# The second half of an output projection, finished tile by tile in every token group instead of the last group alone

## Chip, cores and metric

The kernel runs on one core of a Trainium2 chip. The metric is the time of one execution on the device, in microseconds (us). A kernel is judged by the median of its runs.

## What is computed

One layer of a streaming encoder: norm, a wide input projection, two parallel branches (gated linear attention, gated spatial mixing), their merge, one output projection with a gated residual add, and a final norm. The change touches the end only:

```
    x = x + gate * (merged @ w_out)                  # merged: (tokens, 1024), w_out: (1024, 1024)
    y = rmsnorm(x, final_norm_w)                     # x * rsqrt(mean(x*x) + EPS) * w, float32
```

There are 2,048 prompt tokens and 128 sample tokens, all in float32.

## The kernel before

**Groups and phases.** The 17 tiles of 128 tokens are worked on in three groups: 6 prompt tiles, the sample tile with 4 prompt tiles, and 6 prompt tiles. Each group goes through the phases `h` (input projection), `a` and `b` (the branches' projections) and `o` (output projection, `w_out`). A phase is a list of blocks, a block a list of jobs, and a job is what TensorE (PE) does with one piece of 128 to 512 weight rows. Every float32 operand is split into a high part (`hi`, a cast by ScalarE, ACT) and a rest (`lo`, a subtraction by VectorE, DVE, or GpSimd, POOL), and a product is three matmuls: hi hi, hi lo, lo hi.

**The output projection.** `P.o` has two blocks of kind N (`NJob`), one for each half of the 1,024 output columns. A block has eight jobs, one for each 128 rows of `w_out`. `NJob.tile(j)` issues the three matmuls of one job for token tile j (lines 394 to 396) and adds them up in that tile's PSUM bank. In the order before, `mm` runs all tiles of a job before the next job, so that all the banks of a block are complete only with job 7. The last block of the program (`blocks[-1]`) is the exception: its jobs 4 to 7 are held back and then run tile by tile, each tile with four jobs one after the other, and each tile is finished at once.

**Emptying a bank.** `out_fin(n)(j, ps)` multiplies the bank by the gate (line 1522, DVE), adds that to the residual x in tile `y` (line 1524, DVE for even j, POOL for odd j), and sums the squares (`y_square`, line 1548, ACT): at once for the first half, and for the second half in the generator `y_gen`.

**Who sets the order.** The order is written by a Python planner. `run_all` goes through the jobs: `flush` empties the banks of the job before, `prepare(n)` issues the casts and subtractions for the weights of the jobs n+2 and n+3, `feed(n)` issues weight loads as far as nine weight buffers reach, `job.mm()` issues the matmuls, and `job.then` holds what follows a job. Each engine executes its own instructions in the order in which they were issued. Work beside the matmuls sits in generators in the list `side`, and `step()` advances the first of them between matmuls. `out_before(0)` drains that list before the output projection.

**Fills of the next group.** In phase `h` the next group needs seven combinations of its operands (`AOPS`, in the order S1, A11, S2, S4, A12, S3, A22), each as hi and lo in a pair of large buffers (`U`, 18 in all). `fill_h` casts each combination (line 160, ACT) and subtracts (line 161, the first half of the columns on DVE, the second on POOL). The fills hang on the `then` lists of the output projection's jobs: behind job 1 of its second half the fourth, behind job 3 the fifth (A12), behind job 5 the sixth (S3), behind job 7 the last (A22). Each of these takes over the buffers of two jobs that have just ended.

**The final norm.** Behind the second half, `out_after` puts `y_gen` in front of the next group's matmuls: one step loads the norm's weights, a step for each tile sums the squares, one step reduces them (line 1563, DVE) and takes the root on POOL (lines 1564 and 1565), and then, one step later, each step scales and stores one tile (`y_out`, line 1543, DVE). The next group's first blocks `ga[0]` and `v` are of kind S (`SJob`): 12 matmuls a job (lines 326 to 328) with seven jobs. Four banks are used; jobs 4 to 6 add to banks that `evac` has first read. That is the copy on ACT (line 338) and the sums on DVE (lines 339 and 342), and `g_fin` (line 1320) takes the results out. Job 4 waits for the copy at 338, job 5 for the sum at 342, job 6 for the sum at 1320 that reads job 5's bank. The sum at 342 is in `SJob.evac`:

```
            elif i == 2:
                bk["u2"] = CT(h)
                dve.tensor_tensor(bk["u2"], bk["Q"], bk["t"], ALU.add)
```

Below, b0 is the first block of the next group, b0.5 its job 5, b1.0 the first job of the next block, which runs between b0.5 and b0.6. The boundary is the moment at which b0.0 starts.

Of the kernel before, what the change touches and what calls it, by code (L numbers as in the profile page):

```python
# [13 lines left out]
ALU = mybir.AluOpType  # L14
# [84 lines left out]
LEAD = 2  # L99
# [8 lines left out]
def _fast_body(tc, nc, ctx, io):  # L108
    pe, act, dve, pool, sync = nc.tensor, nc.scalar, nc.vector, nc.gpsimd, nc.sync
# [53 lines left out]
    def mm(out, lhs, rhs, start=True, stop=True):  # L163

        ops = [(a, b) for n, a in enumerate(lhs) for m, b in enumerate(rhs) if n + m < 2]
        for n, (a, b) in enumerate(ops):
            pe.matmul(out, a, b, start=start and n == 0, stop=stop and n == len(ops) - 1)  # L167
# [214 lines left out]
    class NJob(Job):  # L382
# [5 lines left out]
        def tile(self, j):  # L388
# [6 lines left out]
            pe.matmul(bk[j], a, self.w[:, 1], start=False, stop=False)  # L395
            pe.matmul(bk[j], b, self.w[:, 0], start=False, stop=i == 7)  # L396

        def mm(self):
            blk, nt = self.blk, self.blk.ops.h // 64
            if blk is not blocks[-1] or self.i < 4:  # L400
                for j in range(nt):
                    self.tile(j)
                    if j % 2:
                        step()
            elif self.i == 7:
                for j in range(nt):
                    for job in blk.jobs[4:8]:
                        job.tile(j)
                    blk.fin(j, blk.banks[j])

        def evac(self):
            if self.i == 7 and self.blk is not blocks[-1]:
                for j in range(self.blk.ops.h // 64):
                    self.blk.fin(j, self.blk.banks[j])

    class Blk:


        def __init__(self, kind, src, fin, after=None, before=None):
            self.src, self.fin, self.after, self.before = src, fin, after, before  # L420
            self.raw, self.tmp, self.banks = [], {}, {}
            cls, n = {"S": (SJob, 7), "P": (PJob, 4), "N": (NJob, 8)}[kind]
            self.kind, self.jobs, self.kept, self.num = kind, [cls(self, i) for i in range(n)], False, None
            self.ntiles = 4 if kind == "N" else 2
# [10 lines left out]
    def step():  # L435
        rate[1] += rate[0]
        while rate[1] >= 1.0:
            rate[1] -= 1.0
            side.step()

    blocks, jobs, feed_q, feed_n, staged = [], [], [], [0], set()
# [27 lines left out]

    def feed(n, most=4):  # L470

        own = sum(1 for job in jobs[max(n, 0):max(0, n + LEAD + 2)] if not (job.blk.kind == "S" and job.blk.kept))
        while feed_n[0] < len(feed_q):
            live = [f for f in feed_q[:feed_n[0]] if f[3] > n]
            _, fn, args, _ = feed_q[feed_n[0]]
            raw = sum(1 for f in live if f[2])
            if len(live) + own >= NW or (args and raw >= most):
                break
            fn(*args)
            feed_n[0] += 1  # L480
# [24 lines left out]
    def run_all(first):  # L505
        for n, job in list(enumerate(jobs))[first:]:
            flush()
            if job.i == 0 and job.blk.before:
                job.blk.before()
            prepare(n)  # L510
            keep(n + 1)
            feed(n)
            job.mm()
            last[0] = job
            for fn in job.then:
                fn()


    class Steps:
# [433 lines left out]
    def make_group(g):  # L953

        tiles = groups[g]
        nt = len(tiles)
# [539 lines left out]
        def out_before(n):  # L1496
            def f():
                if n == 0:
                    side.drain()
                    cur["yss"] = sm1.tile([128, NTM, 4], F32, tag="xss", name=nm("yss"))  # L1500
                    cur["y"] = {}
                cs = slice(512 * n, 512 * n + 512)
                if n and g + 1 == NG:
                    cur["yw"] = norm_w()
                cur["gate"] = {}
                for k in sorted({t[0] for t in tiles}):
                    cur["gate"][k] = S(512)
                    sync.dma_start(cur["gate"][k], gate_d[k][:, cs])
                for j in range(0, nt, 3):
                    y = U([3, 512])  # L1510
                    for a, b, src in x_rows(g, 512 * n, 512):
                        a2, b2 = max(a, j), min(b, j + 3)
                        if a2 < b2:
                            sync.dma_start(y[:, a2 - j:b2 - j, :], src[:, a2 - a:b2 - a, :])
                    for i in range(j, min(nt, j + 3)):
                        cur["y"][n, i] = y[:, i - j, :]
            return f

        def out_fin(n):
            def f(j, ps):  # L1520
                t, y = S(512), cur["y"][n, j]
                dve.tensor_tensor(t, ps, cur["gate"][tiles[j][0]], ALU.mult)  # L1522
                final = n and g + 1 == NG
                (pool if j % 2 and not final else dve).tensor_tensor(y, y, t, ALU.add)
                if n == 0 or final:
                    y_square(n, j)
                if final:
                    if j > 0:
                        y_tile(j - 1)
                    if j + 1 == nt:  # L1530
                        y_tile(j)
            return f
# [14 lines left out]
        def y_square(n, j):  # L1547
            act.activation(K1("sq", 512, BF16), cur["y"][n, j], AF.Square, accum_out=cur["yss"][:, j, n:n + 1])
# [6 lines left out]

        def y_gen():
            ws = norm_w()
            for j in range(nt):
                yield
                y_square(1, j)  # L1560
            yield
            r = sm1.tile([128, NTM], F32, tag="xrs", name=nm("yrs"))
            dve.tensor_reduce(r[:, 0:nt], cur["yss"][:, 0:nt, 0:2], AX.X, ALU.add)
            pool.tensor_scalar(r[:, 0:nt], r[:, 0:nt], 1.0 / D, EPS, ALU.mult, ALU.add)
            pool.tensor_tensor(r[:, 0:nt], r[:, 0:nt], neghalf.broadcast_to([128, nt]), ALU.pow)
            yield
            for n in range(2):
                for j in range(nt):
                    y_out(n, j, r[:, j:j + 1], ws[n])
                    yield  # L1570
                done.add(("y", g, 2 * n + 2))

        def out_after(n):
            if n and g + 1 < NG:
                return lambda: side.push(y_gen())
# [4 lines left out]
        P = Group()  # L1580
# [12 lines left out]
        P.a = [Blk("P", io["wpa"][:, 2048 * kp:2048 * kp + 2048], pa_fin(kp), None, pa_before(kp)) for kp in range(4)]  # L1593
        P.b = [Blk("P", io["wpb"][:, 2048 * kp:2048 * kp + 2048], pb_fin(kp), None, pb_before(kp)) for kp in range(4)]
        P.o = [Blk("N", io["wo"][:, 4096 * n:4096 * n + 4096], out_fin(n), out_after(n), out_before(n)) for n in range(2)]
        for num, blk in enumerate(P.h):
            blk.kept, blk.num = g > 0, num
        for ph in (P.h, P.a, P.b, P.o):
# [1273 lines left out]
```

## Time and profile before

| what | us |
|---|---|
| median of the runs shown | 2215.55 (2213.68 to 2215.86, 3 runs) |
| the profiled execution, own time | 2220.29 |
| its span in the profile | 2218.5 |
| PE busy in it | 2161.4 (97%) |
| DVE, ACT, POOL busy | 1174.3, 778.6, 678.1 |

The busy shares say that PE is the engine to look at. What a change can win or lose is the idle time of PE at the place of the change, so the views of use are the waits of PE by window, the timelines of the engines around the two boundaries between groups, and the granted clock there. Idle time of the others counts only where PE waits for them.

### The profile page before, as it was taken

How to read it: one execution, taken by the hardware profiler on the slowest of the kernel's cores; microseconds unless marked ns; L12 is line 12 of the kernel's file. 1: busy time of each engine (PE TensorE's matmuls, PEld its weight loads, DVE VectorE, ACT ScalarE, POOL GpSimd, SP SyncE). 2: the span in 40 equal slices, each digit the busy share in tenths (PEclk: the TensorE clock that was granted, in tenths of full speed). 3: DMA queues.
4: the chain of work that ended last, by engine and by line, in shares of the span. 5: the costliest groups of instructions: out<-in, count | busy, mean ns of one | idle time of the engine just before them, and what ended most of it. 6: DMA issues, size and time to landing. Idle time of an engine off the chain costs nothing. (4 is left out here: it accounts for less than half of the span.)

```text
span 2218.5 us, 35445 instructions
## 1 busy us (share of the span) xinstructions
PE 2161.4 (97%) x13165; PEld 2086.5 (94%) x13165; DVE 1174.3 (53%) x2257; ACT 778.6 (35%) x1626; POOL 678.1 (31%) x673
## 2 busy tenths in 40 slices
PE   7899999999989999999999999999999999999998
PEld 4899999999989989999999999989999999999996
DVE  6677787566446545555435236663444434324444
ACT  5445464433344332333311044433333321104322
POOL 0445556436535621111101225620111100222232
PEclk9999999999999999999999999999999999999999
DMA  7777777978975559888889886677777787675332
GB/s 306 291 286 288 295 281 284 349 270 309 342 270 195 174 196 344 279 295 300 290 312 303 298 295 223 230 279 277 222 233 241 239 273 239 220 253 189 122 100 101
DMA packets 191718, 570.91 MB, mean 257 GB/s; under 512 B 21297, under 2 KB 54705, under 8 KB 191537
## 3 DMA queue, kind: packets, MB, share of 16 engines
q1 hardware_dynamic: 186304, 560.36, 72.0%
q10 hardware_dynamic: 5040, 7.68, 1.2%
q8 instruction: 106, 1.74, 0.3%
q14 instruction: 76, 0.61, 0.1%
q0 software_dynamic: 192, 0.52, 0.1%
HBM read 396.38 MB, written 172.10 MB: 256 GB/s over the span
## 5 line engine op out<-in xcount | busy, mean ns | idle before, releaser
L326 PE MATMUL pg<-u,w 128*128 128x384 f32 (+1 forms) x2688 | 902.1, 336 | 15.3 <-DVE c L1320 4.9
L328 PE MATMUL pg<-u,w 128*128 128x384 f32 (+1 forms) x2688 | 880.1, 327 | 3.0 <-DVE w L315 1.9
L327 PE MATMUL pg<-u,w 128*128 128x384 f32 (+1 forms) x2688 | 879.4, 327 | 2.7 <-DVE u L748 2.7
L326 PEld LDWEIGHTS pg<-u,w 128*128 128x128 f32 x2688 | 507.5, 189 | 30.0 <-issue 11.0
L327 PEld LDWEIGHTS pg<-u,w 128*128 128x128 f32 x2688 | 507.7, 189 | 3.9 <-DVE u L748 3.2
L328 PEld LDWEIGHTS pg<-u,w 128*128 128x128 f32 x2688 | 506.6, 188 | 3.7 <-DVE w L315 2.2
L371 PE MATMUL pg<-u,w 128*128 128x384 f32 (+1 forms) x768 | 251.9, 328 | 0.0
L373 PE MATMUL pg<-u,w 128*128 128x384 f32 (+1 forms) x768 | 250.5, 326 | 1.1 <-DVE w L266 1.1
L372 PE MATMUL pg<-u,w 128*128 128x384 f32 (+1 forms) x768 | 250.5, 326 | 0.0
L266 DVE TENSOR_TENSOR w<-wr,w 128x512 fp32r<-128x512 f32 x144 | 159.8, 1128 | 60.6 <-ACT w L263 60.5
L373 PEld LDWEIGHTS pg<-u,w 128*128 128x128 f32 x768 | 144.5, 188 | 1.3 <-DVE w L266 1.3
L371 PEld LDWEIGHTS pg<-u,w 128*128 128x128 f32 x768 | 144.5, 188 | 0.5
L372 PEld LDWEIGHTS pg<-u,w 128*128 128x128 f32 x768 | 144.5, 188 | 0.5
L197 POOL TENSOR_SCALAR st<-st 128x1 f32<-128x1 f32 x74 | 17.3, 234 | 396.9 <-ACT sq L1130 396.3
L263 ACT CAST w<-wr 128x512 fp32r<-128x512 f32 x144 | 87.6, 616 | 141.7 <-PE pg L373 71.6
L338 ACT COPY c<-pg 128x384 f32<-128x384 f32 (+1 forms) x96 | 44.3, 461 | 202.3 <-PE pg L328 184.8
L395 PE MATMUL pg<-w,u 128*128 128x512 f32 x272 | 105.9, 389 | 0.0
L396 PE MATMUL pg<-w,u 128*128 128x512 f32 x272 | 105.8, 389 | 0.0
L394 PE MATMUL pg<-w,u 128*128 128x512 f32 x272 | 105.8, 389 | 0.0
L1157 ACT CAST kn<-pat 128x128 fp32r<-128x128 f32 x68 | 18.1, 267 | 247.6 <-DVE c L1154 247.5
L339 DVE TENSOR_TENSOR c<-pg,c 128x384 f32<-128x384 f32 (+1 forms) x96 | 51.1, 532 | 101.7 <-ACT c L338 97.8
L309 ACT CAST w<-wt 128x512 fp32r<-128x512 f32 x128 | 78.7, 621 | 72.6 <-POOL wt L290 19.7
(236 smaller groups left out, 3157.8 us busy)
## 6 DMA issues: line engine op xcount, KB each, us to landing
wr<-wb SPq DMA_DIRECT2D x64, 512.0 KB, 5.0
w<-wk_0f SPq DMA_DIRECT2D x64, 512.0 KB, 4.4
w<-wk_1f SPq DMA_DIRECT2D x64, 512.0 KB, 4.6
w<-wk_2f SPq DMA_DIRECT2D x64, 512.0 KB, 4.6
w<-wk_3f SPq DMA_DIRECT2D x64, 512.0 KB, 4.4
w<-wk_4f SPq DMA_DIRECT2D x64, 512.0 KB, 4.4
w<-wk_5f SPq DMA_DIRECT2D x64, 512.0 KB, 4.4
w<-wk_6f SPq DMA_DIRECT2D x64, 512.0 KB, 4.9
```

The source lines that it names most:

```text
L263: act.copy(self.w[:, 0], self.src())
L266: dve.tensor_tensor(self.w[:, 1], self.src(), self.w[:, 0].bitcast(F32), ALU.subtract)
L309: act.copy(self.w[:, 0].rearrange("p (k c) -> p k c", k=4), self.src())
L326: pe.matmul(out, w[:, 0, k, :], hi[:, k, :], start=i < 4 and k == 0, stop=False, **kw)
L327: pe.matmul(out, w[:, 0, k, :], lo[:, k, :], start=False, stop=False, **kw)
L328: pe.matmul(out, w[:, 1, k, :], hi[:, k, :], start=False, stop=k == 3, **kw)
L371: pe.matmul(out, w[:, 0, e, c], hi[:, e, ts], start=first, stop=False)
L372: pe.matmul(out, w[:, 0, e, c], lo[:, e, ts], start=False, stop=False)
L373: pe.matmul(out, w[:, 1, e, c], hi[:, e, ts], start=False, stop=end)
L394: pe.matmul(bk[j], a, self.w[:, 0], start=i == 0, stop=False)
L395: pe.matmul(bk[j], a, self.w[:, 1], start=False, stop=False)
L396: pe.matmul(bk[j], b, self.w[:, 0], start=False, stop=i == 7)
```

## The change

Which blocks run their last four jobs tile by tile is now told by a mark, `final`, set on the second half of the output projection of every group. Between the tiles of that loop, `step()` is called, and the `then` lists of jobs 4 to 6 (the fills) run behind tiles 1, 2 and 3. `feed` reserves four weight buffers throughout those jobs. All adds of the second half go to DVE, the squares follow each tile at once, and `y_gen` has no steps for them, but three pauses in place of one behind the root.

```diff
+        def tail(self):
+            return self.blk.final and self.i > 3
         def mm(self):
-            if blk is not blocks[-1] or self.i < 4:
+            if not self.tail():
...
                     for job in blk.jobs[4:8]:
                         job.tile(j)
                     blk.fin(j, blk.banks[j])
+                    if j % 2:
+                        step()
+                        step()
+                    if 0 < j < 4:
+                        for fn in blk.jobs[3 + j].then:
+                            fn()
         def evac(self):
-            if self.i == 7 and self.blk is not blocks[-1]:
+            if self.i == 7 and not self.tail():
...
     def feed(n, most=4):
-        own = sum(1 for job in jobs[max(n, 0):max(0, n + LEAD + 2)] if not (job.blk.kind == "S" and job.blk.kept))
+        own = 4 if 0 <= n and jobs[n].blk.final and jobs[n].i > 3 else sum(1 for job in jobs[max(n, 0):max(0, n + LEAD + 2)] if not (job.blk.kind == "S" and job.blk.kept))
...
-            for fn in job.then:
-                fn()
+            if job.i == 7 or not (job.blk.final and job.i > 3):
+                for fn in job.then:
+                    fn()
...
                 final = n and g + 1 == NG
-                (pool if j % 2 and not final else dve).tensor_tensor(y, y, t, ALU.add)
-                if n == 0 or final:
-                    y_square(n, j)
+                (pool if j % 2 and not n else dve).tensor_tensor(y, y, t, ALU.add)
+                y_square(n, j)
...
         def y_gen():
             ws = norm_w()
-            for j in range(nt):
-                yield
-                y_square(1, j)
-            yield
...
-            yield
+            for _ in range(3):
+                yield
             for n in range(2):
...
+        P.o[1].final = True
```

How the order of the instructions moves is shown at three places of group 0's end. Group 1's end moves alike.

**PE, second half of the output projection, from job 4 on.** The names w1528, w1534, w1535 and w1541 are the weights of jobs 4, 5, 6 and 7; pg1522 and pg1523 are the banks of tiles 0 and 1. Before:

```order
L394 MATMUL pg1522_8552<-w1528_8576,u1460_8181 128x512
L395 MATMUL pg1522_8552<-w1528_8576,u1460_8181 128x512
L396 MATMUL pg1522_8552<-w1528_8576,u1461_8182 128x512
L394 MATMUL pg1523_8556<-w1528_8576,u1460_8181 128x512
L395 MATMUL pg1523_8556<-w1528_8576,u1460_8181 128x512
```

Changed (lines are those of the changed file here and below; up to line 396 they are the same):

```order
L394 MATMUL pg1522_8552<-w1528_8576,u1460_8181 128x512
L395 MATMUL pg1522_8552<-w1528_8576,u1460_8181 128x512
L396 MATMUL pg1522_8552<-w1528_8576,u1461_8182 128x512
L394 MATMUL pg1522_8552<-w1534_8609,u1460_8181 128x512
L395 MATMUL pg1522_8552<-w1534_8609,u1460_8181 128x512
L396 MATMUL pg1522_8552<-w1534_8609,u1461_8182 128x512
L394 MATMUL pg1522_8552<-w1535_8630,u1478_8316 128x512
L395 MATMUL pg1522_8552<-w1535_8630,u1478_8316 128x512
L396 MATMUL pg1522_8552<-w1535_8630,u1479_8317 128x512
L394 MATMUL pg1522_8552<-w1541_8663,u1478_8316 128x512
L395 MATMUL pg1522_8552<-w1541_8663,u1478_8316 128x512
L396 MATMUL pg1522_8552<-w1541_8663,u1479_8317 128x512
```

The weights of job 7 are now read by the tenth to twelfth matmul behind job 3, where they were read by the 55th.

**ACT, from the fifth fill (u1537) to the copy at line 338.** u1544 (changed: u1549) and u1550 (changed: u1559) are the sixth and the last fill, sq the squares. Before:

```order
L160 CAST u1537_8653<-s1532_8603 128x640
L160 CAST u1537_8653<-s1533_8607 128x640
L263 CAST w1541_8663<-wr1497_8437 128x512
L160 CAST u1544_8707<-s1539_8657 128x640
L160 CAST u1544_8707<-s1540_8661 128x640
L160 CAST u1550_8757<-s1546_8711 128x640
L160 CAST u1550_8757<-s1547_8715 128x640
L1548 ACTIVATE sq1563_8802,yss1467_8282<-u1519_8545 128x512
```

Changed, behind the same cast of w1541 and the squares of tiles 0 to 2:

```order
L160 CAST u1549_8720<-s1539_8657 128x640
L160 CAST u1549_8720<-s1540_8661 128x640
L1558 ACTIVATE sq1554_8745,yss1467_8282<-u1520_8547 128x512
L1558 ACTIVATE sq1556_8762,yss1467_8282<-u1520_8547 128x512
L1558 ACTIVATE sq1558_8779,yss1467_8282<-u1520_8547 128x512
L160 CAST u1559_8781<-s1551_8724 128x640
L160 CAST u1559_8781<-s1552_8728 128x640
L338 COPY c1572_8835<-pg1571_8820 128x320
```

The sixth fill now stands between the squares of tile 2 and tile 3, and the last fill, which stood ahead of all squares, behind all of them.

**DVE, from the last fill's subtraction to the second sum of b0.** Line 1522 is the gate's product, 1543 the scaling of the norm; in the changed file these are 1533 and 1553. Before:

```order
L161 TENSOR_TENSOR u1551_8758<-s1546_8711,u1550_8757 128x640
L1522 TENSOR_TENSOR s1552_8763<-pg1522_8552,s1518_8543 128x512
...
L1522 TENSOR_TENSOR s1557_8778<-pg1527_8572,s1518_8543 128x512
L339 TENSOR_TENSOR c1569_8824<-pg1560_8785,c1568_8823 128x320
L342 TENSOR_TENSOR c1574_8846<-pg1571_8829,c1569_8824 128x320
L1563 TENSOR_REDUCE yrs1578_8865<-yss1467_8282 128x6
```

Changed:

```order
L161 TENSOR_TENSOR u1560_8782<-s1551_8724,u1559_8781 128x640
L1569 TENSOR_REDUCE yrs1569_8808<-yss1467_8282 128x6
L1553 SCALAR_TENSOR_TENSOR u1469_8285<-u1469_8285,yrs1569_8808,s1567_8804 128x512
L339 TENSOR_TENSOR c1573_8836<-pg1566_8797,c1572_8835 128x320
L1553 SCALAR_TENSOR_TENSOR u1469_8285<-u1469_8285,yrs1569_8808,s1567_8804 128x512 x2
L342 TENSOR_TENSOR c1576_8858<-pg1575_8841,c1573_8836 128x320
```

The sums 339 and 342 stood ahead of the norm's reduction; now the reduction and three scalings, which need the root, stand ahead of the sum 342.

## Rows read from the trace of the kernel before

**Rows 1.** The page, part 1: busy time, share of the span, instructions.

```profile
PE 2161.4 (97%) x13165; PEld 2086.5 (94%) x13165; DVE 1174.3 (53%) x2257; ACT 778.6 (35%) x1626; POOL 678.1 (31%) x673
```

**Rows 2.** Who TensorE waited for, 800 to 850 us: total, times, longest.

```profile
PE pg L326 <- DVE c L1320: 2.4, 1, 2.4
PE pg L326 <- DVE c L342: 0.8, 1, 0.8
PE pg L326 <- ACT c L338: 0.2, 1, 0.2
```

**Rows 3.** The same view, 1470 to 1500 us.

```profile
PE pg L326 <- DVE c L1320: 1.5, 1, 1.5
```

**Rows 4.** Windows: us; busy PE, PEld, DVE, ACT, POOL; granted clock; DMA share; GB/s.

```profile
846.80:850.30 3.50, 3.50 (x16) 3.50 (x15) 3.50 (x7) 0.00 (x0) 0.00 (x0) 0.51 0.92 298
...
1488.00:1491.50 3.50, 3.50 (x22) 3.50 (x21) 2.29 (x4) 0.43 (x1) 0.00 (x0) 1.00 1.00 331
...
2180.00:2207.00 27.00, 27.00 (x121) 22.36 (x120) 14.67 (x23) 6.88 (x17) 4.95 (x13) 1.00 0.31 116
```

**Rows 5.** Timeline of ACT: start, us, line, operation, idle before.

```profile
812.74 1.36 ACT L160 CAST u<-s 128x640 fp32r<-128x640 f32 x2 [3.34 <-PE pg L395]
```

**Rows 6.** Timeline of DVE beside it.

```profile
813.50 0.82 DVE L161 TENSOR_TENSOR u<-s,u 128x640 fp32r<-128x640 f32 x1 [4.76 <-ACT u L160]
814.24 2.65 DVE L266 TENSOR_TENSOR w<-wr,w 128x512 fp32r<-128x512 f32 x2
```

**Rows 7.** Timeline of PE beside it.

```profile
812.76 0.39 PE L394 MATMUL pg<-w,u 128*128 128x512 f32 x1
...
815.03 0.39 PE L395 MATMUL pg<-w,u 128*128 128x512 f32 x1
```

**Rows 8.** Timeline of ACT at the second boundary.

```profile
1457.98 1.76 ACT L160 CAST u<-s 128x768 fp32r<-128x768 f32 x2 [2.79 <-DMA s<-h2A120f]
```

**Rows 9.** Timeline of DVE at the second boundary.

```profile
1459.73 2.93 DVE L266 TENSOR_TENSOR w<-wr,w 128x512 fp32r<-128x512 f32 x2
```

**Rows 10.** Timeline of PE at the second boundary.

```profile
1456.67 0.39 PE L394 MATMUL pg<-w,u 128*128 128x512 f32 x1
```

**Rows 11.** Timeline of ACT behind the last job of group 0.

```profile
829.05 1.36 ACT L160 CAST u<-s 128x640 fp32r<-128x640 f32 x2 [6.80 <-PE pg L395]
832.71 0.63 ACT L1548 ACTIVATE sq<-u 128x512 bf16<-128x512 f32 x1 [2.29 <-DVE u L1524]
```

**Rows 12.** Timeline of DVE behind the last job of group 0.

```profile
831.28 1.39 DVE L1524 TENSOR_TENSOR u<-u,s 128x512 f32<-128x512 f32 x1
...
842.37 2.74 DVE L1543 SCALAR_TENSOR_TENSOR u<-u,yrs,s 128x512 f32<-128x512 f32 x4 [1.35 <-POOL yrs L1565]
845.03 0.48 DVE L1320 TENSOR_TENSOR c<-pg,c 128x320 f32<-128x320 f32 x1
```

**Rows 13.** Timeline of POOL behind the last job of group 0.

```profile
830.54 1.58 POOL L161 TENSOR_TENSOR u<-s,u 128x640 fp32r<-128x640 f32 x1 [6.64 <-ACT u L160]
...
840.70 0.21 POOL L1564 TENSOR_SCALAR yrs<-yrs 128x6 f32<-128x6 f32 x1 [1.04 <-DVE yrs L1563]
841.00 1.34 POOL L1565 TENSOR_TENSOR yrs<-yrs,nhf 128x6 f32<-128x6 f32 x1
```

**Rows 14.** Timeline of PE, group 1's first blocks.

```profile
829.08 0.30 PE L326 MATMUL pg<-u,w 128*128 128x320 f32 x1
829.23 0.31 PE L327 MATMUL pg<-u,w 128*128 128x320 f32 x1
```

**Rows 15.** Timeline of POOL behind the last job of group 1.

```profile
1471.95 1.85 POOL L161 TENSOR_TENSOR u<-s,u 128x768 fp32r<-128x768 f32 x1 [4.97 <-ACT u L160]
```

**Rows 16.** The page, part 6: a weight's load: count, KB, us to landing.

```profile
w<-wk_5f SPq DMA_DIRECT2D x64, 512.0 KB, 4.4
```

**Rows 17.** Timeline of DVE in the last group's tile loop.

```profile
2194.68 0.69 DVE L1524 TENSOR_TENSOR u<-u,s 128x512 f32<-128x512 f32 x1
2196.67 0.69 DVE L1522 TENSOR_TENSOR s<-pg,s 128x512 f32<-128x512 f32 x1 [1.30 <-PE pg L396]
```

More of the change, by code (lines that the diff above doesn't have):

```diff
@@ L420, in __init__ @@
             self.src, self.fin, self.after, self.before = src, fin, after, before
-            self.raw, self.tmp, self.banks = [], {}, {}
+            self.raw, self.tmp, self.banks, self.final = [], {}, {}, False
             cls, n = {"S": (SJob, 7), "P": (PJob, 4), "N": (NJob, 8)}[kind]
```

## The prediction

> **What bounds the kernel now.** I read the page first: TensorE (PE) is busy for 97% of the span [rows 1], so a gain can only come out of PE's idle time, and a loss is whatever idle time the change adds. Then I read the waits of PE in windows around the two places that change, the boundaries between groups. At the first boundary PE waits 0.2, 0.8 and 2.4 us [rows 2], all for the next group's first block: its banks are read late, because ACT and DVE are still busy emptying the output projection's six banks. At the second there is one wait of 1.5 us [rows 3]. The windows show a further cost: behind the wait of 2.4 us the granted clock falls from 1.00 to 0.51, from 2.4 to 1.2 GHz, for 3.5 us, and behind the wait of 1.5 us it stays at 1.00 [rows 4]. At 0.51 of the clock 3.5 us lose up to 1.7 us; by the count it is 1.2, since PE has 16 records there where 3.5 us hold 24 matmuls of 0.147 us [rows 14]. I take 1.5, between the two. The idle time that the change can win back is therefore 3.4 + 1.5 + 1.5 = 6.4 us, 0.3% of the time. A measurement of this kernel can tell about 0.2%, or 4.4 us, from no change.
>
> The second thing to see is how tight the weights' preparation is. PE runs one matmul of this projection every 0.227 us (2.27 us for ten, [rows 7]), and nothing waits there, because a job takes 18 of them.
>
> **The change, part by part.** The matmuls are the same in number and kind. In the last group, whose order is the same in both kernels, the tile loop runs without a gap: PE is busy for 27.00 us of 27 [rows 4]. So the order itself costs nothing; what counts is what the other engines do beside it.
>
> *Side steps between tiles, the reserve in `feed`.* The list of side work is empty there (it is drained at the start of the projection, and the norm's generator comes after it), so the new steps do nothing. Job 5 of the next block gets its weights later, when the last tile's first matmuls have ended, some 2 us ahead of the boundary; a load lands after 4.4 us [rows 16], 2.4 us behind the boundary, and they are due 8.8 us behind it (below). Zero, and 6 us of cover.
>
> *The weights of jobs 6 and 7, first boundary.* These are now needed by the eighth and the eleventh matmul behind job 3 and no longer by the 37th and the 55th. Their `lo` halves stand on DVE behind the fifth fill, and that fill waits for job 3's last matmuls, since it takes over their buffers. The rows of before show this chain, which does not move: the cast starts at 812.74 [rows 5], DVE's part of the fill at 813.50, and the two `lo` halves run from 814.24 to 816.89 [rows 6]. The first matmul of job 4 starts at 812.76 and the eleventh at 815.03 [rows 7]. That one must now wait until 816.9: **1.9 us**, in two parts of about 1.2 and 0.7. Bounds: at 0.69 us for each half, as DVE takes for this size where POOL is quiet [rows 17], it is 0.6; with a fall of the clock, 3.4. I take the row itself.
>
> *The same, second boundary.* Here the fill's data comes late: the cast waits for a DMA until 1457.98 [rows 8], and the two `lo` halves end at 1459.73 + 2.93 = 1462.66 [rows 9]. The first matmul of job 4 starts at 1456.67 [rows 10], the eleventh 2.27 later, at 1458.94. It waits **3.7 us**, nearly 3 of them in one piece. That is longer than the 2.4 us behind which the clock fell, so I add **1.5**. Bounds: with the data in time (1.3 us earlier) and quick halves 0.9, with no loss of clock; 5.2 otherwise.
>
> *The fills in the loop.* The sixth fill is issued behind tile 2 and takes the buffers of jobs 4 and 5. These jobs now read them until the last tile, so ACT stops there until the sixth matmul of the last tile ends, 1.2 us ahead of the boundary B (seven times 0.227, less a duration of 0.39, [rows 7]). I let the cast start at B - 1.4, since PE's ends are modelled. DVE starts 0.76 later, and its next instruction another 0.74 behind [rows 5, 6]: B + 0.1. Everything behind the fill, products, adds and squares of tiles 3 to 5, waits with it. Then the chain is, in order: product 0.7, add 1.4 beside POOL's fill [rows 12], two products and adds at 0.65 to 0.7 each [rows 17], B + 4.8; a square, 0.63 [rows 11] and some 0.2 for reading out its sum, B + 5.6; the two casts of the last fill, 1.36 [rows 11], B + 7.0; POOL's part of that fill, 1.58 [rows 13], which stands ahead of the root on POOL, B + 8.6; the root and the scaling ahead of it, 0.21 and 1.34 with gaps of 0.1 [rows 13], B + 10.3; then on DVE a scaling of the norm, the sum 339, two more scalings and the sum 342, 3 x 0.68 + 2 x 0.48 [rows 12], **B + 13.3**. Only then may job 5 of b0 start. It is due after five jobs of 12 matmuls at 0.147 us [rows 14], at B + 8.8.
>
> So at the first boundary job 4 waits 0.4 us for the copy behind the casts (B + 7.0 + 0.4 against 7.0), job 5 another 4.1, and job 6, behind six more scalings and two sums of DVE (5.05 us) against 24 matmuls (3.5), another 1.5: **6.0 us** in place of 3.4. One fall of the clock follows in each kernel and cancels out.
>
> At the second boundary the group has five tiles, so one product and add less (1.35 us), but casts and POOL's part are longer (0.2 and 0.3 us, [rows 8, 15]) and so is the first add (0.25 as an estimate, since POOL is busy that much longer): B + 12.9. The next group's matmuls have 384 columns for 320, so by the rows an estimate of 0.174 us each: job 5 is due at B + 10.4 and waits 2.5, job 6 about 0.9: **3.4 us** in place of 1.5.
>
> *Adds from POOL to DVE, squares at once.* Three adds and then two leave POOL, whose add next to these takes about twice the 0.69 us of DVE [rows 17]; their time on DVE is in the chain above. For tiles 0 to 2 all is hidden under the later tiles.
>
> *The pause.* Three steps lie behind the root for one, and the steps of the squares are gone, so the scalings are issued within b0's evacuation and no longer behind the sum 342. The pause costs nothing by itself, but it is too short: with no scaling ahead of them, the sums 339 and 342 could follow the copy (B + 7.4) and end at about B + 8.4, in time.
>
> The Trainium skill's page "GPSIMD Engine Reference", section "Engine selection", puts elementwise adds on VectorE and not on GpSimd. By that alone the five moved adds would be a gain of about 3 us; the trace agrees on the two durations, but here it is DVE's line that PE waits for [rows 2, 3], so the sum goes by the rows.
>
> **Sum.** First boundary 1.9 + 6.0 - 3.4 = +4.5; second 3.7 + 1.5 + 3.4 - 1.5 = +7.1; together +11.6 us. On the profiled execution's 2220.3 that gives 2231.9. It lies 4.7 above the median of the runs, 2215.55, so I forecast **2227 us**, slower by 0.5%.
>
> **Rivals.**
> *The boundary clears, faster.* If the banks of all tiles were emptied under the loop, all 6.4 us would be won: 2209. For it: the last group's loop leaves PE no gap [rows 4], and tiles 0 to 2 are surely finished early. Against it: the last group has no fills, and here the sixth stands ahead of tiles 3 to 5. It decides if ACT's wait for the buffers is not there, that is, if the cast of that fill starts well before the last tile. The Trainium skill's page "TensorE: Matmul & The Clock Gate", section "Loop structure matters more than you think", stands on this side: it calls it good to run all pieces of one output tile and to copy it out while the next tile's matmuls follow. No run here yet shows that order with fills in it. 0.07.
> *Both costs small, no change.* The `lo` halves are quick and the fill's data in time (0.6 and 0.9), and the chain is a microsecond shorter at either end: 0.6 + 1.6 and 0.9 + 0.9 give +4 us, 2219.5. Against it: the chain's waits are fixed by the order. 0.15.
> *The clock falls more often.* If two more of the new waits cost a low clock (1.5 each: the first boundary's weights, the second's job 5) and each chain is a microsecond longer, it is 11.6 + 3 + 2 = +16.6: 2232. Whether 1.9 in two parts or 2.5 is enough lies between the 1.5 and 2.4 us that rows show. 0.15.
> *The change does nothing there.* The order of the instructions shows that it does. Under 0.01.
>
> **How the numbers follow.** The forecast has 0.62 and lies between 2220 and 2230; with the rival above it, slower by over 0.2% (beyond 2220.0) has 0.77. No change (2211.1 to 2220.0) has 0.16, faster 0.07. For 8 in 10 the range reaches from 2217, inside the no-change case, to 2232.
>
> **What would show it.** Right: PE waits for a `lo` half on DVE (line 266) at the eighth and eleventh matmul behind job 3, about 2 us in group 0 and 3 to 4 in group 1, the latter with a granted clock near 0.5 behind it; ACT idle for some 4 us ahead of the sixth fill's cast, which starts near the end of the last tile; the root on POOL ends some 10 us behind the boundary; PE waits 3 to 5 us at b0.5 for the sum 342. Wrong: no wait in the loop, or the sum 342 done by B + 9. If the waits are there and the time is not longer, something later gives it back, and PE's idle time in the next 100 us should then be less than before.

## The result, and the profile after

The changed kernel takes **2228.43 us** (median of 4 runs, 2227.57 to 2232.5). The kernel before took 2215.32 beside it, so the ratio is **1.0058**, with a 95% interval of 1.0046 to 1.0070: slower by 13 us. Run again for the experiments, the ratio was 1.0048 (1.0034 to 1.0061). The forecast was 2227 us, and the chance of 0.77 stood on slower.

The profiled execution has 2228.42 us of its own and a span of 2226.6. The profile of before lay 4.7 us above its median and this one lies on its median, so the two spans differ by 8.1 us only. A difference of two single executions contains what varies elsewhere; at the boundaries themselves it can be read off, which is done below.

The changed file's lines are 1533 for the gate's product, 1535 for the add, 1553 for the scaling, 1558 for the squares, 1331 for the sum that was 1320, and 1569 to 1571 for the reduction and the root.

The page, part 1, of the change (answers to [rows 1]):

```profile
PE 2164.8 (97%) x13165; PEld 2088.8 (94%) x13165; DVE 1173.7 (53%) x2262; ACT 778.3 (35%) x1626; POOL 671.8 (30%) x668
```

PE has the same number of instructions and is busy for 3.4 of the 8.1 us more: the same matmuls, some of them at a lower clock (below). The rest is idle time. Who PE waited for, at the first boundary (800 to 860 us) and at the second (1440 to 1510), as total, times, longest (answers to [rows 2, 3]):

```profile
PE pg L326 <- DVE c L342: 4.0, 1, 4.0
PE pg L395 <- DVE w L266: 1.8, 1, 1.8
...
PE pg L395 <- DVE w L266: 3.0, 2, 1.7
PE pg L326 <- DVE c L342: 2.3, 1, 2.3
PE pg L326 <- DVE c L1331: 0.4, 1, 0.4
```

Line 395 is a matmul of the output projection that waits for a `lo` half, line 326 a matmul of the next group's first block. Both kinds of wait that the prediction named are there, and the waits of [rows 2, 3] are gone: 5.8 us for 3.4, and 5.7 us for 1.5. The windows, with the granted clock behind the five busy times (answers to [rows 4]):

```profile
814.00:817.40 3.40, 3.40 (x9) 2.60 (x9) 1.66 (x3) 0.00 (x0) 0.00 (x0) 0.53 0.43 154
...
841.00:848.00 7.00, 4.47 (x17) 4.47 (x18) 7.00 (x13) 0.32 (x1) 0.00 (x0) 0.54 0.78 277
...
1462.50:1469.30 6.80, 5.54 (x14) 4.16 (x14) 2.81 (x3) 0.72 (x2) 0.88 (x1) 0.52 0.42 140
...
1490.00:1495.00 5.00, 3.99 (x23) 3.99 (x24) 5.00 (x9) 0.48 (x1) 0.00 (x0) 1.00 0.96 296
```

Around the two boundaries the clock is at 1.2 GHz in three places, where it was in one. Behind the wait of 2.3 us at 1491 it stays at 1.00.

**Where the 13 us are.** At the start of the loop the change's trace runs 2.56 us ahead of the one before (the fifth fill's subtraction on DVE starts at 810.94 for 813.50, [rows 6]). Behind the boundary, where the orders meet again, it is 2.11 us behind, by the same kind of comparison: +4.7 us. At the second boundary the distance goes from 1.6 to 9.3 us: +7.7. Together that is +12.4 us; the forecast had +4.5 and +7.1.

**The wait in the loop.** PE's timeline at the loop's start in group 0, and then in group 1:

```profile
811.57 0.39 PE L394 MATMUL pg<-w,u 128*128 128x512 f32 x1
813.77 0.50 PE L395 MATMUL pg<-w,u 128*128 128x512 f32 x1 [1.81 <-DVE w L266]
...
814.87 0.63 PE L395 MATMUL pg<-w,u 128*128 128x512 f32 x1
...
1461.76 0.50 PE L395 MATMUL pg<-w,u 128*128 128x512 f32 x1 [1.74 <-DVE w L266]
...
1463.99 0.79 PE L395 MATMUL pg<-w,u 128*128 128x512 f32 x1 [1.26 <-DVE w L266]
```

In group 0 a single wait is listed where the prediction had two parts, 1.2 and 0.7. The reason is in DVE's two subtractions, which the timeline shows as one pair of 2.63 us. Grouped by line they come apart (nanoseconds: shortest, median, longest; first of group 0, then of group 1):

```profile
L266 DVE TENSOR_TENSOR w<-wr,w x2: 678/1353/2028, 811.7 to 813.6; 128x512 fp32r<-128x512 f32 x2
...
L266 DVE TENSOR_TENSOR w<-wr,w x2: 686/1500/2315, 1461.0 to 1461.6; 128x512 fp32r<-128x512 f32 x2
```

In group 0 the first takes 2.03 us, while POOL's part of the fill runs beside it (811.61 to 813.16), and the second 0.68. Job 6 waits for the long one, and by then job 7's half is nearly done. In group 1 it is the second that runs beside POOL's part (1461.12 to 1463.39) and takes 2.32 us, so both jobs wait.

**The chain behind the boundary.** In group 0 the boundary B is at 830.25, the start of b0.0. ACT, then DVE, POOL and PE (answers to [rows 11 to 14]):

```profile
828.86 1.36 ACT L160 CAST u<-s 128x640 fp32r<-128x640 f32 x2 [4.29 <-PE pg L395]
...
835.19 0.63 ACT L1558 ACTIVATE sq<-u 128x512 bf16<-128x512 f32 x1 [0.60 <-DVE u L1535]
...
835.82 1.34 ACT L160 CAST u<-s 128x640 fp32r<-128x640 f32 x2
```

```profile
840.61 0.75 DVE L1553 SCALAR_TENSOR_TENSOR u<-u,yrs,s 128x512 f32<-128x512 f32 x1 [3.14 <-POOL yrs L1571]
841.27 0.48 DVE L339 TENSOR_TENSOR c<-pg,c 128x320 f32<-128x320 f32 x1
841.68 1.40 DVE L1553 SCALAR_TENSOR_TENSOR u<-u,yrs,s 128x512 f32<-128x512 f32 x2
843.00 0.48 DVE L342 TENSOR_TENSOR c<-pg,c 128x320 f32<-128x320 f32 x1
...
837.29 1.57 POOL L161 TENSOR_TENSOR u<-s,u 128x640 fp32r<-128x640 f32 x1 [5.40 <-ACT u L160]
838.94 0.21 POOL L1570 TENSOR_SCALAR yrs<-yrs 128x6 f32<-128x6 f32 x1
839.23 1.34 POOL L1571 TENSOR_TENSOR yrs<-yrs,nhf 128x6 f32<-128x6 f32 x1
...
843.53 0.63 PE L326 MATMUL pg<-u,w 128*128 128x320 f32 x1 [3.98 <-DVE c L342]
```

The reader sees the chain of the prediction, link by link: the fill's cast starts 1.4 us ahead of B, the casts of the last fill end at B + 6.9, POOL's part at B + 8.6, the root at B + 10.3, the sum 342 at B + 13.2. While POOL takes its part of the fill and the root, DVE is idle for 3.1 us, although the sum 339 has its operands: the scaling in front of it on DVE's queue waits.

### The profile page after: what moved, and what is told of

It is laid out like the page before. It is cut to its first block, busy times and chain, and to the rows that moved or that the text cites. A ratio compares the mean times of both kernels' runs of the same rounds, so it can differ in the third digit from the quotient of the medians.

```text
span 2226.6 us, 35447 instructions
## 1 busy us (share of the span) xinstructions
PE 2164.8 (97%) x13165; PEld 2088.8 (94%) x13165; DVE 1173.7 (53%) x2262; ACT 778.3 (35%) x1626; POOL 671.8 (30%) x668
## 3 DMA queue, kind: packets, MB, share of 16 engines
q8 instruction: 106, 1.74, 0.3%
## 5 line engine op out<-in xcount | busy, mean ns | idle before, releaser
L395 PE MATMUL pg<-w,u 128*128 128x512 f32 x272 | 107.9, 397 | 4.8 <-DVE w L266 4.8
L394 PE MATMUL pg<-w,u 128*128 128x512 f32 x272 | 107.5, 395 | 0.0
L396 PE MATMUL pg<-w,u 128*128 128x512 f32 x272 | 107.5, 395 | 0.0
```

Source lines behind the costliest of these rows:

```text
L394: pe.matmul(bk[j], a, self.w[:, 0], start=i == 0, stop=False)
```

## Experiments

The ratios below are those of each run to the kernel before, timed on the same chip (about 2218 us there). To compare with the change, its 1.0058 is taken; 0.001 is 2.2 us. The change's second ratio, 1.0048, was measured on the chip of the first four runs; by it each gain over the change is 2.2 us smaller, and both are given where it matters.

**The fifth fill behind the loop's first tile.** Its place on ACT and DVE is then behind the `lo` halves of jobs 6 and 7.

```
-                    if 0 < j < 4:
+                    if j < 4:
...
-            if job.i == 7 or not (job.blk.final and job.i > 3):
+            if job.i == 7 or not (job.blk.final and job.i > 2):
```

> The change, with the fifth fill (job 3's) issued behind tile 0 of the loop, so that the lo halves of the weights of jobs 6 and 7 no longer stand behind it on DVE. My theory: the waits in the loop (1.8 us in group 0, 3.0 us in group 1) and the low clock behind each of them go, 7 to 9 us less than the change: 2219 to 2222. Rival: the loop's waits only bring forward a wait that comes at the boundary anyway, because the fills and the norm's root set the time there: the waits go, but the time stays within 2 us of 2228.

Ratio 1.0020 (1.0011 to 1.0029), that is 8.4 us less than the change (6.2 by 1.0048). PE's waits in the same two windows:

```profile
PE pg L326 <- DVE c L342: 4.0, 1, 4.0
...
PE pg L326 <- DVE c L342: 2.3, 1, 2.3
```

The waits of the loop are gone, those for the sum 342 stand unchanged, and the clock is at 1.00 from 812 to 820 and from 1460 to 1470. Behind the wait of 2.3 us, however, the clock now falls (0.61 from 1479.6 to 1484.0, some 1.6 us), where it stayed at 1.00 in the change. So the late `lo` halves, with the two low clocks behind them, cost 6 to 8 us net of that fall; the change's own trace has some 9.7 us for them.

**Ten pauses behind the root for three.**

```
-            for _ in range(3):
+            for _ in range(10):
```

> The change, with ten pauses behind the root for three, so that the sums 339 and 342 of the next group's first block stand ahead of the norm's scalings on DVE. My theory: the wait at b0.5 (4.0 us, then 2.3) goes with its low clock, 7 to 10 us less than the change: 2218 to 2222. Rival: DVE has too much to do at the boundary in any order, and the scalings then hold up the second block's sums: at most 3 us less, 2225 or more.

Ratio 1.0008 (0.9999 to 1.0017), 11 us less than the change (9 by 1.0048). The mirror image, PE's waits at the first boundary and at the second:

```profile
PE pg L395 <- DVE w L266: 1.8, 1, 1.8
...
PE pg L395 <- DVE w L266: 3.3, 2, 2.0
```

Now the sums 339 and 342 run ahead of the first scaling (339 starts at 837.87), nobody waits for them, and the clock is at 1.00 from 836 to 850:

```profile
838.47 0.49 DVE L342 TENSOR_TENSOR c<-pg,c 128x320 f32<-128x320 f32 x1
840.96 1.41 DVE L1553 SCALAR_TENSOR_TENSOR u<-u,yrs,s 128x512 f32<-128x512 f32 x2 [1.41 <-POOL yrs L1571]
```

Nothing else moved: counted from the boundary, here at 830.61, the sixth fill's cast (B - 1.4) and the root's end (B + 10.3) are as late as in the change. So the wait at b0.5 is DVE's order and not the late root by itself.

**The fills of jobs 4 to 6 behind the loop.**

```
-                    if 0 < j < 4:
-                        for fn in blk.jobs[3 + j].then:
-                            fn()
+                for k in (4, 5, 6):
+                    for fn in blk.jobs[k].then:
+                        fn()
```

> The change, with the sixth fill behind the tile loop and not behind tile 2. My theory: ACT and DVE no longer stop for its buffers ahead of tiles 3 to 5, so these are emptied under the loop; the root then waits for two fills' worth of POOL's work, ends some 1 to 2 us earlier, and the wait at b0.5 shrinks by as much at each boundary: 2 to 4 us less, 2224 to 2226. Rival, in which the stop for the buffers is the whole cost at the boundary: the wait at b0.5 goes, 7 us or more less.

Ratio 1.0059 (1.0045 to 1.0073): nothing won, and the theory missed. The tiles are emptied as it said, one after the other under the loop. Counted from the boundary, here at 831.41, the last add on DVE ends at B + 1.6, where the change has B + 4.8. DVE's timeline behind that, and POOL's:

```profile
832.33 0.69 DVE L1535 TENSOR_TENSOR u<-u,s 128x512 f32<-128x512 f32 x1
...
842.47 0.75 DVE L1553 SCALAR_TENSOR_TENSOR u<-u,yrs,s 128x512 f32<-128x512 f32 x1 [4.95 <-DMA s<-final_norm_w]
...
835.17 3.71 POOL L161 TENSOR_TENSOR u<-s,u 128x640 fp32r<-128x640 f32 x2 [20.84 <-ACT u L160]
```

Two things took the gain. On POOL both parts of the fills now run in a row, and of the 3.2 us the root behind them keeps 1.1: it ends at B + 9.2, for B + 10.3 in the change. That much the theory had. But the scaling then waits for the norm's weights and starts at B + 11.1, for B + 10.4. How long their two loads took from issue to landing (shortest, median, longest), in the change and here:

```profile
DMA to landing us min/median/max: 5.6/5.9/6.1
```

```profile
DMA to landing us min/median/max: 7.9/8.3/8.6
```

They were issued as far behind the boundary as in the change (2.4 us) and took 2.4 us longer. What crowds them was not tried; the weights of the next blocks are issued around them in both kernels. The wait for the sum 342 grew to 5.0 and 3.6 us. That DVE's order is what matters was then put to the test by this edit together with the pause (below).

**No tile loop in the first two groups.** Only the mark is taken back; the adds on DVE, the squares at once and the pause stay.

```
-        P.o[1].final = True
+        P.o[1].final = g + 1 == NG
```

> The change without its tile loop in groups 0 and 1 (job by job as before), but with the adds on DVE, the squares at once and three pauses. My theory: no wait for weights, but all six tiles are emptied behind the last job, behind two fills, and the sum 342 stands behind the root: a wait of 6 to 8 us at b0.5 in group 1 and 3 to 5 in group 2, slower than before by 6 to 11 us: 2221 to 2226. Rival, in which the tile loop is all that harms: no slower than before, 2215.

Ratio 1.0042 (1.0029 to 1.0056), slower by 9 us. The size is as expected, the place is not. PE's waits at the first boundary, and ACT there:

```profile
PE pg L326 <- ACT c L338: 4.2, 1, 4.2
PE pg L326 <- DVE c L342: 1.1, 1, 1.1
PE pg L326 <- DVE c L1331: 1.0, 1, 1.0
```

```profile
836.51 0.63 ACT L1558 ACTIVATE sq<-u 128x512 bf16<-128x512 f32 x1 [0.60 <-DVE u L1535]
...
837.13 0.41 ACT L338 COPY c<-pg 128x320 f32<-128x320 f32 x1
```

The squares, issued at once, stand ahead of the copy at 338 on ACT's queue, and job 4 of b0 waits for that copy behind six of them, each 1.3 us behind the last, as DVE's products and adds end. The copy starts 10.9 us behind the boundary; in the kernel before it stood behind three squares and started 7.0 us behind it. The generator's steps, which the change removed, let it pass there. So, by this trace, the squares' new place has a price in the order without the loop. What the loop would do with the squares and the adds in their old places was not run.

**The two edits that gained, together.** The fifth fill behind tile 0 and ten pauses.

> The change with the two edits that each gained alone: the fifth fill behind the loop's first tile, and ten pauses behind the root for three. Theory (the two losses lie in different places and add up): ratio to the kernel before 1.0058 - 0.0038 - 0.0050 = 0.9970, faster by 6 to 7 us, which is PE's idle time and low clock at the boundaries of the kernel before (6.4 us on record); PE waits neither for a lo half nor for the sum 342, and the granted clock stays at 1.00 through both boundaries. Rival (the waits overlap, what one edit takes away comes back at the next tight place): no better than the pause alone, 1.0000 to 1.0010, with a new wait of PE in the next 100 us.

Ratio 0.9977 (0.9968 to 0.9987), run again on another chip as the last run below 0.9968 (0.9957 to 0.9979): **faster than the kernel before** by 5 and 7 us. The two losses add up. Of all PE's waits from 790 to 870 us one is left, and from 1430 to 1520 none:

```profile
PE pod L1009 <- DMA u<-waldf: 0.5, 1, 0.5
```

That wait was not there before: it is for a load that takes over a buffer of the norm's output, and whose issue on SP waited 1.5 us for stores of that output. The granted clock is at 1.00 throughout both boundaries.

**All three edits.**

> The change with three edits at once: the fifth fill behind the loop's first tile, ten pauses behind the root for three, and the fills of jobs 4 to 6 behind the loop for between its tiles. Moving the fills alone gave nothing (1.0059 beside the change's 1.0058), because the scaling then waited for the norm's weights, and the sum 342 for the scaling. Theory (the wait at b0.5 is DVE's order and the loop's wait is the late lo halves; the place of the sixth fill matters only through that order): with the pause the fills' place is worth nothing more, so the ratio to the kernel before is that of the first two edits alone, 0.997 (change 1.0058, less 0.0038 for the first, less 0.0050 for the second), within 0.001 of the run without the third edit. Rival (three fills in a row behind the loop hold ACT up for the copy at 338, which job 4 of b0 waits for): PE waits 1 to 2 us for ACT's copy at each boundary, ratio 0.998 to 0.999.

Ratio 0.9990 (0.9981 to 0.9999). That is the rival's ratio and not the theory's. With the pause, the fills behind the loop do no great harm, and they win nothing; the intervals of this and the run without them meet, so a loss of 3 us isn't settled. The rival's place was wrong: no wait for the copy. PE's waits at the first boundary:

```profile
PE pod L1012 <- DMA u<-waldf: 1.4, 1, 1.4
PE pg L326 <- DVE c L1334: 1.0, 1, 1.0
```

The second is again the norm's weights: two scalings, which waited 3.9 us for them, stand ahead of that sum on DVE.

**The kernel before with four pauses for one.**

```
-            yield
+            for _ in range(4):
+                yield
             for n in range(2):
```

> The kernel before with a single edit: four pauses behind the root for one. The tile loop, the fills, the adds and the squares stay as they were. Theory (the waits of 2.4 and 1.5 us at the boundaries of the kernel before are DVE's scalings ahead of the sum that job 6 of b0 needs, and not the banks of six tiles that are all complete at once): these two waits go, and the low clock behind the first, 2.4 + 1.5 + 1.5 = 5.4 us: ratio 0.9976, between 0.9970 and 0.9985; PE still waits 0.8 and 0.2 us for the sum 342 and the copy 338. Rival (the late banks of the output projection themselves hold the sum up, so that only an earlier emptying, tile by tile, helps): the waits stay, ratio 0.9995 to 1.0005.

Ratio 0.9986 (0.9977 to 0.9995), just outside the range expected, and clear of the rival's. PE's waits at the first boundary:

```profile
PE pg L326 <- DVE c L342: 0.8, 1, 0.8
PE pod L998 <- DMA u<-waldf: 0.5, 1, 0.5
PE pg L326 <- DVE c L1320: 0.4, 1, 0.4
PE pg L326 <- ACT c L338: 0.2, 1, 0.2
```

Of the 2.4 us of [rows 2] 0.4 is left, the 1.5 us of [rows 3] is gone, and with them the low clock of [rows 4]. So these waits of the kernel before were DVE's scalings as well, and not the six banks that come at once. Those, which DVE and ACT empty first, can be behind the 0.8 and the 0.2 only, which have not moved.

**The kernel before with ten pauses, and the two edits again.**

> The kernel before with ten pauses behind the root for one. Four pauses left waits of 0.8, 0.4 and 0.2 us at the first boundary and none at the second. Theory (DVE's order alone): the 0.4 us goes too, since no scaling stands ahead of the sum 1320 any more; ratio 0.998 to 0.999, within 0.001 of the run with four pauses. Rival (the scalings and stores, made later still, hold up the next load that takes over their buffers): PE waits over 1 us for a DMA near 865 us, ratio 0.9995 or more.

> The change with the fifth fill behind the loop's first tile and ten pauses, once more, beside the kernel before with ten pauses. Theory (with the pause right, the tile loop only takes away the last waits of about 1 us at the first boundary, and the waits near 865 us for a load are common to both): ratio 0.9970 to 0.9985, within 0.001 of the kernel before with ten pauses, so that the loop itself is worth nothing that can be told. Rival (tile by tile is worth its own gain): lower than the kernel before with ten pauses by 0.0015 or more, intervals apart.

Ratios 0.9984 (0.9975 to 0.9993) and 0.9968 (0.9957 to 0.9979). The waits at the first boundary in the one, and the only one in the other:

```profile
PE pod L998 <- DMA u<-waldf: 1.1, 1, 1.1
PE pg L326 <- DVE c L342: 0.8, 1, 0.8
PE pg L326 <- ACT c L338: 0.2, 1, 0.2
```

```profile
PE pod L1009 <- DMA u<-waldf: 1.1, 1, 1.1
```

Once the pause is right, the loop takes away 1.0 us of waits that the profile shows. The two comparisons, with the run of four pauses on one chip and of ten on the other, give it 0.0009 and 0.0016, 2 to 3.5 us; the intervals overlap in the one and just meet in the other. So the second run's theory (0.9970 or more, within 0.001) is missed, and its rival (intervals apart) is not reached. That the loop is worth that much stays open, and with it come the adds on DVE and the squares at once, which were not told apart from it here. The rival of the first of these two runs had a wait of over 1 us for a DMA: it came, with 1.1 us and in both orders alike, and the gain is there all the same.

**The odd tiles' adds back on POOL.**

```
-                (pool if j % 2 and not n else dve).tensor_tensor(y, y, t, ALU.add)
+                (pool if j % 2 and not (n and g + 1 == NG) else dve).tensor_tensor(y, y, t, ALU.add)
```

> The change with the adds of odd tiles back on POOL in the first two groups, as they were in the kernel before. Theory (the adds are hidden under the loop except those of the last two or three tiles, and the place of the add moves the root by at most 1.4 - 0.7 us for each of them): within 2 us of the change either way, ratio 1.0049 to 1.0067. Rival (elementwise adds cost twice on POOL, and the root stands behind them on the same engine): slower than the change by 3 us or more, 1.0072 and above, with the wait for the sum 342 longer by 1.5 us at each boundary.

Ratio 1.0064 (1.0050 to 1.0077): no difference from the change that can be told. The wait for the sum 342 is 3.9 us for 4.0 at the first boundary and 2.8 for 2.3 at the second. At the first, POOL's two adds take 3.0 us behind the boundary, but DVE goes on beside them, and the last ends at B + 4.6 for B + 4.8 in the change; the root ends at B + 10.3 in both. At the second the root ends 0.5 us later than in the change (B + 10.3 for B + 9.8), behind a single add of 1.7 us on POOL.

**The change again.**

> The change itself, unaltered, beside the kernel before on the same chip. Theory (its loss is 12 to 13 us of waits and low clock at the two boundaries): ratio 1.0050 to 1.0066. The clock behind the first boundary's wait of 1.8 us in the loop is open: it fell in one profile of the change and stayed at 1.00 behind a wait of the same length when the odd tiles' adds were on POOL. If it is that the wait of 1.8 us always costs a low clock in this order, this profile shows about 0.5 from 814 to 817 us again; if it is at the edge, 1.00 may stand there, with the second wait of about 1 us in its place. Rival for the ratio (the first measurement was lucky in its kernel before): 1.003 or less.

Ratio 1.0048 (1.0034 to 1.0061), a hair under the range, and the clock fell again behind the first boundary's wait in the loop, to 0.57 from 816.5 to 819.9 us.

## Why the prediction was right, step by step

- *What bounds the kernel now.* The reading of the kernel before put all its waits down to the six banks. For the 2.4 and 1.5 us that was wrong: with four pauses, and the banks as late as ever, 0.4 and nothing of them are left. The sum took these waits as rows and does not hang on it.
- *The weights' `lo` halves, first boundary.* The sum had 1.9 us in two parts of 1.2 and 0.7, without a fall of the clock. Measured: 1.8 in one piece. **The clock then fell**, which the prediction had only as a bound and in the rival "the clock falls more often". The 11 intervals from 813.77 to 817.98, up to 0.43 us for 0.23, took 1.7 us more than at full clock. The step that failed is the split into halves of equal length: the pair of 2.65 us in [rows 6] was 2.05 and 0.68, as the same grouping of lines shows in the kernel before:

```profile
L266 DVE TENSOR_TENSOR w<-wr,w x2: 680/1366/2052, 814.2 to 816.2; 128x512 fp32r<-128x512 f32 x2
```

- *The same, second boundary.* 3.7 us with 1.5 for the clock; measured 3.0 us, in two pieces of 1.74 and 1.26, and the 13 intervals behind them, up to 0.59 us for 0.23, took 2.7 us more. "Nearly 3 in one piece" was wrong in the same way; the sum of both terms, 5.2 on record, is 5.7.
- *The fill ahead of tiles 3 to 5.* Right to 0.1 us at every link (the cast at B - 1.4, the root at B + 10.3, the sum 342 at B + 13.2 for 13.3; at the second boundary B + 12.9, as forecast). The wait at job 5 is 4.0 for 4.1 us, and 2.35 for 2.5.
- *Jobs 4 and 6 of b0.* Forecast 0.4 and 1.5 us at the first boundary. Job 4 came 0.24 us late (837.53 behind 837.14, for 0.147), which the listing leaves out; job 6 did not wait, and at the second boundary it waited 0.4 for 0.9. Here "one fall of the clock follows in each kernel and cancels out" was too simple: behind the wait of 4.0 us 16 matmuls ran at intervals of 0.267 us, so the 24 that lie ahead of job 6 took some 5.8 us for 3.5, until 849.30, and its sum, done at 848.25, was in time. The low clock cost 2.2 us there, 0.7 more than in the kernel before, in place of the wait of 1.5.
- *The sum.* +4.7 and +7.7 for +4.5 and +7.1. The terms missed in both directions by up to 2 us, and the clock, under-rated at the first boundary's weights and behind job 5, was made up for by the wait of 1.5 that it hid. That the total came within 1 us is in part luck.
- *The pause "is too short".* Right: with ten pauses the sum 342 ends at B + 8.4, as written, and 9 to 11 us go. The interval of that difference is about 3 us either way; the trace of the change has 9.4 us (waits of 4.0, 2.35 and 0.44, a low clock of 2.2, and 0.15 us for each wait that the listing, which counts from the end of the matmul before, leaves out).
- *Adds and side steps at nothing.* Nothing in the runs speaks against either: the adds made no difference that can be told. The Trainium skill's page "GPSIMD Engine Reference", section "Engine selection", which puts such adds on VectorE, agrees with the durations, 1.3 to 1.7 us on POOL for 0.69 on DVE alone. In time it is neither borne out nor contradicted: with the adds on POOL the root came no later at the first boundary, where DVE worked on beside them, and 0.5 us later at the second.
- *The rival "the boundary clears, faster", 2209.* It asked for the order of the fills to be no obstacle, and in the change it was one. With the fifth fill behind tile 0 and the pause at ten its time came, though not its way: no wait at either boundary, and 5 and 7 us won for the 6.4 on record. The sign that the rival named, the sixth fill's cast well before the last tile, is not there; the cast still starts 1.4 us ahead of the boundary, which is at 829.17 in that run:

```profile
827.79 1.36 ACT L160 CAST u<-s 128x640 fp32r<-128x640 f32 x2 [4.18 <-PE pg L395]
```

The Trainium skill's page "TensorE: Matmul & The Clock Gate", section "Loop structure matters more than you think", calls for finishing one output tile while the next is computed. In that run the trace agrees (clock at 1.00 through both boundaries), in the change it does not (1.2 GHz in three places). But ten pauses in the old order reach 0.9984, so half of the gain or more needs no loop.

## What to carry to other kernels

Reordering matmuls so that each output is complete early moves the *last* weights' due time forward and holds all their buffers to the end; move the preparation of those weights ahead of whatever else shares its engines, before judging the new order. An engine's queue is a line: put nothing that waits for a slow chain (here a scaling behind a root) in front of a short sum that the bottleneck waits for, and count how many steps it must be held back. Before a pair of instructions is split into halves in a sum, look at each one's duration.

## What the runs showed of the hardware

The fall of PE's clock does not go by the length of the wait alone. Behind a wait of 1.81 us at the same matmul it fell in the change, in its repetition, in the run with ten pauses and in the run with the fills behind the loop, and it did not in the run with the adds on POOL. PE's timeline there, to be held against the change's above:

```profile
814.42 0.50 PE L395 MATMUL pg<-w,u 128*128 128x512 f32 x1 [1.81 <-DVE w L266]
...
815.22 0.40 PE L395 MATMUL pg<-w,u 128*128 128x512 f32 x1
```

Behind the wait for the sum 342 at the second boundary it stayed at 1.00 in the change (2.35 us), in its repetition (2.34) and with the adds on POOL (2.84), and it fell with the fifth fill moved (2.34). In the five runs with the wait of 1.81 us PE was busy without a gap, at 1.00, from 800 to 811. What decides is open; a price for a wait of about 2 us should carry 0 and 1.7 us as its two ends.

A subtraction of 128x512 on DVE took 0.68 to 0.69 us alone, 2.03 to 2.05 beside POOL's subtraction of 128x640, and 2.32 to 2.33 beside one of 128x768. A single instruction can be three times as long while another engine works beside it; why is not shown here.
